# A transformer trunk on one core: the second quarter of attention goes first, filler products on both sides of the fifth block, one lasting tile of scores, adding transfers spread over stage A

## The chip, the cores and the metric

The kernel runs on one core of a Trainium2 chip. A core has four compute engines that run side by side, each with its own stream of instructions: TensorE (PE in the profile; its weight loads are PEld), VectorE (DVE), ScalarE (ACT) and GpSimd (POOL). SyncE (SP) issues most of the DMA transfers between the device's memory and the core's SBUF; GpSimd issues some. Matmul results land in PSUM. An engine takes its instructions in order, and waits on semaphores for the other engines and for transfers.

The metric is the device time of one execution in microseconds (us), as the median of several runs.

## The reference

One layer over 2048 positions of width 1024, 16 heads of 64, all float32: chunked attention with a learned position bias, then a dense SwiGLU part of width 2816, each between two RMS norms and added to the residual.

```python
def chunk_relpos_attention(h, w_qkv, w_o, rel_bias):
    """Chunked attention: chunk c attends to chunks max(0,c-8)..c."""
...
    for c in range(n_chunks):
        k0 = max(0, (c - LEFT_CHUNKS) * CHUNK)
        k1 = (c + 1) * CHUNK
...
        sc = jnp.einsum('bhqd,bhkd->bhqk', q_blk, k[:, :, k0:k1]).astype(jnp.float32) * scale
        sc = sc + bias[None, :, :, BAND - n_keys:]
        p = jax.nn.softmax(sc, axis=-1).astype(v.dtype)
        outs.append(jnp.einsum('bhqk,bhkd->bhqd', p, v[:, :, k0:k1]))
...
    return merge_heads(o) @ w_o
...
        h = rms_norm(x, g_pre_mix[i])
...
        x = x + rms_norm(m, g_post_mix[i])
        h = rms_norm(x, g_pre_ffn[i])
        x = x + rms_norm(swiglu(h, w_gate[i], w_up[i], w_down[i]), g_post_ffn[i])
```

A chunk is 64 positions (`CHUNK`) and `LEFT_CHUNKS` is 8, so 128 queries see at most 640 keys: their own 128 and the 512 before. The first 512 positions of the sequence see fewer, since nothing stands before them.

## The kernel before

Every product that needs float32 is made of three matmuls on parts of the operands (`products`, L197 to L199): one product unit is three matmuls of 128x512.

**Stage A** (`project()`, TensorE from 0 to 492 us of the profiled execution) makes v, q and k for all positions in blocks that take fewer products than a plain matrix product, at the price of sums of weights and of activations. It is a generator of 672 product units, and the main program counts them in `done`. Results q, k, v go to device memory and are fetched again by attention. Beside it the main program advances `weight_sums()`, a generator that prepares sums of the feed-forward part's down weights in device memory with 44 copies and 44 adding transfers of 256 KB: the copies (`copy`) are issued by SP, the adding ones (`add`) by GpSimd, in 60 steps. GpSimd also stores sums of weights for stage A itself (tiles `s_q_S`) and computes the norms' small powers (tiles `hr`).

**Stage B**, attention, runs from 492 to 1139.5 us. A job, `Attend(n, p)`, is a quarter n of the positions (512 queries) and a pair of heads p: 4 x 8 = 32 jobs, in the order of the list `jobs`. A job has four turns of 128 queries. Quarter n=0 sees 128, 256, 384 and 512 keys in its four turns, and the other quarters 640 in each (`self.prev`). A turn's work, by the functions that the main loop calls:
- `scores`: eight matmuls (four where there are few keys) into `st`, one tile over three PSUM banks of which there is one buffer; VectorE adds the bias and finds the row's extreme (head one, then head two), ScalarE takes the exponential of each (tiles `sc`). The loop is three turns ahead with the scores (`AHEAD`).
- `scaled`: VectorE's reciprocal of the row sums, GpSimd's scaling of `sc`.
- `transposed`: TensorE turns four 128x128 blocks of each head into a PSUM tile `tt` (two buffers); VectorE copies head one's into `pT`, ScalarE head two's.
- `fifth`: the fifth block of both heads, which only the quarters with 640 keys have, goes into a third such `tt`, copied by ScalarE.
- `output`, once per job, at the beginning of the next job's first turn: the product with v into `po`.

`load` fetches a job's q, keys, bias, and for every second pair the values v; a job with previous keys fetches those of quarter n-1 as well. It is issued behind the second block of scores of the job before it.

**Filler.** While a quarter's attention runs, `o_quarter` of the quarter before it, the product with w_o, supplies product units (64 in a quarter) that `fill(t)` takes from a generator, so much TensorE time at a time; `left` is what remains. The first quarter of attention has no filler, and the last quarter's `o_quarter` runs after attention. The main loop sets the order of all this on TensorE by hand (`manual_schedule`): the program's order is TensorE's order. On the other engines a planner orders the instructions when the kernel is built, by its own costs.

The lines that set how much filler goes where, before:

```python
        share = (0.4 if t % 4 == 0 else 1.2) * left[0] / max(per - t % per - 1, 1)
        if t > 0 and t % 4 == 0:
            fill(0.45 * share)
...
        fill((0.55 if t % 4 == 0 else 1.0) * share)
        job.fifth()
```

So a job's first turn, which also has the output product, gets a third of what the other turns get, and all filler of a turn stands ahead of its fifth block.

Of the kernel before, what the change touches and what calls it, by code (L numbers as in the profile page):

```python
# [49 lines left out]
def trunk(  # L50
# [344 lines left out]
            return [one(dt) for dt in range(KT)]  # L395

    heads = (slice(0, 64), slice(64, 128))
    phase = {}
    ats, values, osums = {}, {}, {}
    bias = {}  # L400
# [43 lines left out]
    class Attend:  # L444
# [8 lines left out]
        def load(self, begin=False):  # L453
            n, p, ap = self.n, self.p, phase.get("ap")
            if begin:
                both, rest = hb_tile(2), hb_tile(3, F32)
                self.q = both[:, 0]
                self.kk = both[:, 1].rearrange("d a c -> d (a c)").rearrange("d (h c) -> d h c", h=2)
            else:
                self.q = ap.tile([P, 4, HALF], F32R, tag="q", name=f"q_{n}_{p}", bufs=2)  # L460
                self.kk = ap.tile([P, 2, 2 * HALF], F32R, tag="k", name=f"k_{n}_{p}", bufs=2)
            src = q_d[n][p].rearrange("(h d) a c -> d h (a c)", h=2)
            for half in heads:
                sp.dma_start(self.q[half].rearrange("d (h a) c -> d h (a c)", h=2).bitcast(F32), src)
            if self.prev:
                sp.dma_start(self.kk[:, :, 0:HALF].bitcast(F32), k_d[n - 1][p])
            sp.dma_start(self.kk[:, :, HALF:].bitcast(F32), k_d[n][p])
            if begin:
                flat = rest[:, 1].rearrange("d a c -> d (a c)")
                self.bias = [bias_tile(h, h, flat[:, 640 * h : 640 * h + 640]) for h in range(2)]  # L470
            else:
                self.bias = [bias_tile(NH * n + 2 * p + h, 2 * p + h) for h in range(2)]
            if p % 2 == 0:
                here = slice(p * P, p * P + 256)
                if begin:
                    v = rest[:, 0].rearrange("d a c -> d (a c)").rearrange("d (b c) -> d b c", b=8)
                else:
                    v = ap.tile([P, 8, 256], F32, tag="v", name=f"v_{n}_{p}", bufs=2)
                if self.prev:
                    sp.dma_start(v[:, 0:4, :], v_d[n - 1][:, :, here])  # L480
                sp.dma_start(v[:, 4:8, :], v_d[n][:, :, here])
                values[n, p // 2] = v
# [7 lines left out]
        def scores(self, ib):  # L490
# [6 lines left out]
            else:  # L497
                n, k0 = (ib + 1) * P, HALF
                cuts = [(0, n), (512, 512 + n)]
            st = phase["psa"].tile([P, 3 * HALF], F32, tag="S", name="st", bufs=1)  # L500
            for h in range(2):
                c0 = cuts[h][0]
                for a, b in zip(cuts[h][:-1], cuts[h][1:]):
# [58 lines left out]
        def output(self):  # L562
            n, p = self.n, self.p
            v = values[n, p // 2]
            terms = [(0, 4, 0, HALF)]
            for r in range(1, 5 if self.prev else 4):
                if self.prev:
                    terms.append((r, r - 1, 0, r * P))
                if r < 4:
                    terms.append((r, 4 + r, r * P, HALF))  # L570
            po = phase["psa"].tile([P, HALF], F32, tag="po", name="po", bufs=1)
            for m, (r, kb, c0, c1) in enumerate(terms):
                for h in range(2):
                    c = (p % 2) * P + h * 64
                    pe.matmul(  # L575
                        po[heads[h], c0:c1], v[:, kb, c : c + 64], self.pT[:, h, r, c0:c1],
                        start=m == 0, stop=m == len(terms) - 1,
                    )
            if p == 0:
                ats[n] = Cols(((0, 1), (2, 3))[n % 2])  # L580
            act.activation(ats[n].hi(p), po, AF.Copy)
            return lambda: dve.tensor_tensor(ats[n].lo(p), po, ats[n].hi(p).bitcast(F32), op=ALU.subtract)

    def o_quarter(n):

        src = ats[n]
        last = n == NQ - 1
        osums[n] = row_tile("osum", f"osum_{n}") if n % 2 else const.tile([P, HALF], F32, name=f"osum_{n}", tag="osum", bufs=1)
        for d2 in range(KT // 2):
            w = take()  # L590
            if last and d2 == KT // 2 - 1:
# [913 lines left out]
    stack_a, stack_f = ExitStack(), [ExitStack(), ExitStack()]  # L1505
    ctx.enter_context(tc.manual_schedule(engines={mybir.EngineType.PE}))

    jobs = [Attend(n, p) for n in range(NQ) for p in range(NPAIR)]
    open_ffn(0)
    sums_, done = weight_sums(), 0.0  # L1510
    for c in project():
        tick(c / (3 * C512))
        done += c / (3 * C512)
        if done > 400.0 and done % 4.0 < 1.0:
            next(sums_, None)
    drain()
    stack_f[0].close()
# [31 lines left out]
        if t < AHEAD - 1:  # L1549
            jobs[0].scaled()  # L1550
    for t in range(slots):
        share = (0.4 if t % 4 == 0 else 1.2) * left[0] / max(per - t % per - 1, 1)
        if t > 0 and t % 4 == 0:
            fill(0.45 * share)
            low = jobs[t // 4 - 1].output()
            if t % per == 0:
                n = t // per - 1
                fill(1e9)
                drain()
                work, left[0] = o_quarter(n), KT * KT * 3 * C512  # L1560
                if n > 0:
                    later.extend(lates[n - 1].rows(1.5) + lates[n - 1].write(3.0, pool))
                if n == 2:
                    later.extend(blocks[0].sums(2.0))
        if t == 16:
# [7 lines left out]
        ahead(t + AHEAD)  # L1573
        if t > 0 and t % 4 == 0:
            low()
        fill((0.55 if t % 4 == 0 else 1.0) * share)
        job.fifth()
    jobs[-1].output()()
    fill(1e9)
    drain()  # L1580
# [90 lines left out]
```

## Time and profile before

| what | value |
|---|---|
| median of three runs | 2477.16 us (2471.22 to 2478.87) |
| the profiled execution | 2479.19 us, span of its records 2477.4 us |
| mean granted clock of TensorE | 0.986 |
| busy share of the span | TensorE 95%, VectorE 67%, ScalarE 47%, GpSimd 13% |
| memory read and written | 380.14 and 170.44 MB, 222 GB/s over the span |
| matmuls | 11480, 2356.4 us busy |

In the rows of the profile a group is named by its line, engine, operation, and by the tiles it writes and reads (`st<-k,q`); then stand its count, its busy time and mean length, and the idle time of that engine just ahead of it with what ended it. In a timeline a row is the start, the length and the instruction, with the wait ahead of it in brackets. Between one block of scores and the next on TensorE lies one turn, so the distance of two such starts is the length of a turn. The time between two starts of `po`, the output product, is a job.

### The profile page before, as it was taken

What the parts mean: (1) busy time and instruction counts of PE and PEld (TensorE: products, weight loads), DVE (VectorE), ACT (ScalarE), POOL (GpSimd) and SP (SyncE); (2) the same over time, 40 slices, a digit from 0 to 9 for tenths busy, and PEclk for the clock granted to TensorE, in tenths of its full rate; (3) what the DMA queues carried; (4) which work ended last, traced back from release to release, by engine and by line L of the source; (5) the groups of instructions that cost most, each with busy time, mean ns of one, the idle gap of its engine ahead of it and who ended that gap; (6) DMA issues with size and microseconds to landing.
All of it is one profiled execution on the core that took longest, in us unless ns stands there. A gap on an engine that the chain in (4) does not pass through costs nothing.

```text
span 2477.4 us, 33015 instructions
## 1 busy us (share of the span) xinstructions
PE 2356.4 (95%) x11480; PEld 1916.3 (77%) x11480; DVE 1651.3 (67%) x2625; ACT 1163.5 (47%) x2039; POOL 313.6 (13%) x422
## 2 busy tenths in 40 slices
PE   8999999978899899888999999999999999999998
PEld 6888788756667667666887888888888888888887
DVE  7787856656555555566877688577657657555567
ACT  7445633356555555565533343356433333334454
POOL 1000022133223323330000000000000000000002
PEclk9999999988999999999999999999999999999999
DMA  7677599999767877865567554377666757457654
GB/s 281 200 255 258 179 296 322 273 251 241 206 179 203 249 189 196 236 182 197 185 241 248 187 192 157 127 236 236 229 220 195 231 171 226 142 162 241 193 185 155
DMA packets 229782, 529.72 MB, mean 214 GB/s; under 512 B 26320, under 2 KB 42720, under 8 KB 225136
## 3 DMA queue, kind: packets, MB, share of 16 engines
q1 hardware_dynamic: 217712, 480.42, 62.3%
q0 software_dynamic: 11904, 47.19, 6.1%
q8 instruction: 91, 1.49, 0.3%
q14 instruction: 75, 0.61, 0.1%
HBM read 380.14 MB, written 170.44 MB: 222 GB/s over the span
## 4 chain that ended last, share of the span: by engine, by line
PE 54%; DVE 2%; issue 1%; ACT 1%; DMA 1%; POOL 0%; DVEq 0%; SPq 0%; POOLq 0%; ACTq 0%
PE pd L199 6%; PE pd L197 6%; PE pd L198 6%; PE pb L197 5%; PE pb L199 5%; PE pb L198 5%; PE pa L199 3%; PE pa L198 3%; PE pa L197 3%; PE pc L199 3%; PE pc L198 3%; PE pc L197 3%; PE po L575 1%; PE mm L199 1%; PE mm L197 1%
## 5 line engine op out<-in xcount | busy, mean ns | idle before, releaser
L518 ACT ACTIVATE sc<-sc,rows 128x640 f32<-128x640 f32 (+4 forms) x256 | 193.0, 755 | 126.2 <-DVE rows L514 125.9
L530 POOL TENSOR_SCALAR sc<-sc,rows 128x640 f32<-128x640 f32 (+4 forms) x256 | 192.9, 766 | 411.7 <-DVE rows L527 212.4
L514 DVE CUSTOM_DVE_ANT_0 sc<-st,bias 128x640 f32<-128x640 f32 (+2 forms) x248 | 176.1, 745 | 95.8 <-PE st L506 66.1
L197 PE MATMUL pb<-hb,w_wg_T 128*128 128x512 f32 x528 | 206.0, 390 | 2.6 <-DVE terms L963 2.6
L199 PE MATMUL pb<-hb,w_wg_T 128*128 128x512 f32 x528 | 205.7, 390 | 0.0
L198 PE MATMUL pb<-hb,w_wg_T 128*128 128x512 f32 x528 | 205.6, 389 | 0.0
L545 PE MATMUL tt<-ident,sc 128*128 128x128 f32 x928 | 144.1, 286 | 46.1 <-DVE pT L548 25.2
L545 PEld LDWEIGHTS tt<-ident,sc 128*128 128x128 f32 x928 | 107.6, 146 | 82.7 <-issue 68.8
L505 PE MATMUL st<-k,q 128*128 128x384 f32 (+3 forms) x440 | 142.8, 344 | 29.7 <-DVE rows L514 20.0
L199 PE MATMUL pd<-a,w_d_T 128*128 128x512 f32 (+1 forms) x368 | 140.0, 380 | 0.1
L197 PE MATMUL pd<-a,w_d_T 128*128 128x512 f32 (+1 forms) x368 | 140.0, 380 | 0.0
L198 PE MATMUL pd<-a,w_d_T 128*128 128x512 f32 (+1 forms) x368 | 139.9, 380 | 0.0
L197 PE MATMUL pa<-hb,w_wg_B 128*128 128x512 f32 x352 | 137.1, 389 | 0.0
L199 PE MATMUL pa<-hb,w_wg_B 128*128 128x512 f32 x352 | 137.0, 389 | 0.0
L198 PE MATMUL pa<-hb,w_wg_B 128*128 128x512 f32 x352 | 137.0, 389 | 0.0
L506 PE MATMUL st<-k,q 128*128 128x384 f32 (+3 forms) x440 | 131.7, 319 | 0.0
L965 ACT ACTIVATE terms<-terms 128x512 f32<-128x512 f32 x65 | 41.1, 632 | 181.9 <-DVE terms L963 181.9
L548 DVE COPY pT<-tt 128x512 f32<-128x512 f32 (+3 forms) x128 | 81.5, 637 | 66.6 <-PE tt L545 34.5
L131 ACT ACTIVATE w_wg_T<-raw 128x1024 fp32r<-128x1024 f32 x88 | 92.9, 1057 | 70.1 <-PE pa L199 30.8
L354 DVE TENSOR_TENSOR a<-raw_a,a 128x512 fp32r<-128x512 f32 x154 | 105.7, 694 | 28.8 <-ACT a L353 28.3
L575 PE MATMUL po<-pT,v 128*64 128x256 f32 (+3 forms) x864 | 124.6, 436 | 0.0
L289 POOL TENSOR_TENSOR rs<-ms,neg_half 128x4 f32<-128x4 f32 (+1 forms) x7 | 8.4, 1201 | 865.2 <-DVE ms L287 865.2
(265 smaller groups left out, 6226.5 us busy)
## 6 DMA issues: line engine op xcount, KB each, us to landing
raw<-in_w_gu SPq DMA_DIRECT2D x77, 512.0 KB, 4.2
q<-q SPq DMA_DIRECT2D x62, 512.0 KB, 7.5
k<-k SPq DMA_DIRECT2D x55, 512.0 KB, 9.8
s_g_S<-raw POOLq DMA_DIRECT2D x44, 512.0 KB, 3.0
raw_d<-d_S SPq DMA_DIRECT2D x88, 256.0 KB, 3.7
raw_a<-aT SPq DMA_DIRECT2D x88, 256.0 KB, 3.6
raw<-s_g_S SPq DMA_DIRECT2D x44, 512.0 KB, 4.3
bias<-ext_d SPq DMA_DIRECT2D x124, 144.0 KB, 9.9
```

The source lines that it names most:

```text
L131: act.activation(hi, raw, AF.Copy)
L197: pe.matmul(pt, a_hi, b_hi, start=first, stop=False, skip_group_check=go_on)
L198: pe.matmul(pt, a_hi, b_lo, start=False, stop=False, skip_group_check=go_on)
L199: pe.matmul(pt, a_lo, b_hi, start=False, stop=last, skip_group_check=go_on)
L354: eng.tensor_tensor(lo, src, hi.bitcast(F32), op=ALU.subtract)
L505: pe.matmul(st[:, a:b], q[:, 2 * h, cols], kk[:, h, key], start=True, stop=False)
L506: pe.matmul(st[:, a:b], q[:, 2 * h + 1, cols], kk[:, h, key], start=False, stop=True)
L514: dve.tensor_tensor_reduce(out=sc[:, :n], in0=st[:, c0 : c0 + n], in1=rev, scale=-1.0, scalar=3.0e38, op0=ALU.add, op1=ALU.min, accum_out= ...
L518: act.activation(sc[:, :n], sc[:, :n], AF.Exp, bias=nmax, scale=-1.0, accum_out=rows[:, h : h + 1])
L530: last_pool[0] = pool.tensor_scalar(sc[:, :n], sc[:, :n], rows[:, 2 + h : 3 + h], 1.0, op0=ALU.mult, op1=ALU.mult)
L545: pe.transpose(tt[:, u, :], sc[h][:, b * P : b * P + P], ident)
L575: pe.matmul(po[heads[h], c0:c1], v[:, kb, c : c + 64], self.pT[:, h, r, c0:c1], start=m == 0, stop=m == len(terms) - 1,)
```

## The change

Four things. Line numbers of the changed kernel are higher by one to eight.

1. `SEQ_OF = (1, 0, 2, 3)`: attention takes quarter n=1 first and n=0 second. Quarter n=1 now has no filler, and n=0 has n=1's `o_quarter` as filler. n=2 has n=0's, n=3 has n=2's, and n=3's runs after attention, as before. The buffers that alternated by n alternate by the place in the sequence.
2. A turn's filler: the extra factors 0.4 and 1.2 are gone, so each turn has an equal share; half of it stands ahead of the fifth block, and the other half after it, or, in a job's first turn, half ahead of the output product and half ahead of the fifth block.
3. The score tile `st` is allocated once and kept, instead of being taken anew from a pool with one buffer in each turn.
4. `weight_sums()` advances from unit 110 of stage A in every ninth unit, instead of from unit 400 in every fourth.

```diff
--- before.py
+++ after.py
@@ -395,6 +395,7 @@
             return [one(dt) for dt in range(KT)]
 
     heads = (slice(0, 64), slice(64, 128))
+    SEQ_OF = (1, 0, 2, 3)
     phase = {}
     ats, values, osums = {}, {}, {}
     bias = {}
@@ -469,7 +470,7 @@
                 flat = rest[:, 1].rearrange("d a c -> d (a c)")
                 self.bias = [bias_tile(h, h, flat[:, 640 * h : 640 * h + 640]) for h in range(2)]
             else:
-                self.bias = [bias_tile(NH * n + 2 * p + h, 2 * p + h) for h in range(2)]
+                self.bias = [bias_tile(2 * jobs.index(self) + h, 2 * p + h) for h in range(2)]
             if p % 2 == 0:
                 here = slice(p * P, p * P + 256)
                 if begin:
@@ -497,7 +498,9 @@
             else:
                 n, k0 = (ib + 1) * P, HALF
                 cuts = [(0, n), (512, 512 + n)]
-            st = phase["psa"].tile([P, 3 * HALF], F32, tag="S", name="st", bufs=1)
+            if "S" not in phase:
+                phase["S"] = phase["psa"].tile([P, 3 * HALF], F32, name="st", bufs=1)
+            st = phase["S"]
             for h in range(2):
                 c0 = cuts[h][0]
                 for a, b in zip(cuts[h][:-1], cuts[h][1:]):
@@ -577,15 +580,15 @@
                         start=m == 0, stop=m == len(terms) - 1,
                     )
             if p == 0:
-                ats[n] = Cols(((0, 1), (2, 3))[n % 2])
+                ats[n] = Cols(((0, 1), (2, 3))[SEQ_OF.index(n) % 2])
             act.activation(ats[n].hi(p), po, AF.Copy)
             return lambda: dve.tensor_tensor(ats[n].lo(p), po, ats[n].hi(p).bitcast(F32), op=ALU.subtract)
 
     def o_quarter(n):
 
         src = ats[n]
-        last = n == NQ - 1
-        osums[n] = row_tile("osum", f"osum_{n}") if n % 2 else const.tile([P, HALF], F32, name=f"osum_{n}", tag="osum", bufs=1)
+        last = n == SEQ_OF[-1]
+        osums[n] = row_tile("osum", f"osum_{n}") if SEQ_OF.index(n) % 2 else const.tile([P, HALF], F32, name=f"osum_{n}", tag="osum", bufs=1)
         for d2 in range(KT // 2):
             w = take()
             if last and d2 == KT // 2 - 1:
@@ -1505,13 +1508,13 @@
     stack_a, stack_f = ExitStack(), [ExitStack(), ExitStack()]
     ctx.enter_context(tc.manual_schedule(engines={mybir.EngineType.PE}))
 
-    jobs = [Attend(n, p) for n in range(NQ) for p in range(NPAIR)]
+    jobs = [Attend(n, p) for n in SEQ_OF for p in range(NPAIR)]
     open_ffn(0)
     sums_, done = weight_sums(), 0.0
     for c in project():
         tick(c / (3 * C512))
         done += c / (3 * C512)
-        if done > 400.0 and done % 4.0 < 1.0:
+        if done > 110.0 and done % 9.0 < 1.0:
             next(sums_, None)
     drain()
     stack_f[0].close()
@@ -1549,17 +1552,18 @@
         if t < AHEAD - 1:
             jobs[0].scaled()
     for t in range(slots):
-        share = (0.4 if t % 4 == 0 else 1.2) * left[0] / max(per - t % per - 1, 1)
+        share = left[0] / max(per - t % per - 1, 1)
         if t > 0 and t % 4 == 0:
-            fill(0.45 * share)
+            fill(0.5 * share)
             low = jobs[t // 4 - 1].output()
             if t % per == 0:
                 n = t // per - 1
                 fill(1e9)
                 drain()
-                work, left[0] = o_quarter(n), KT * KT * 3 * C512
+                work, left[0] = o_quarter(SEQ_OF[n]), KT * KT * 3 * C512
                 if n > 0:
-                    later.extend(lates[n - 1].rows(1.5) + lates[n - 1].write(3.0, pool))
+                    late = lates[SEQ_OF[n - 1]]
+                    later.extend(late.rows(1.5) + late.write(3.0, pool))
                 if n == 2:
                     later.extend(blocks[0].sums(2.0))
         if t == 16:
@@ -1573,8 +1577,10 @@
         ahead(t + AHEAD)
         if t > 0 and t % 4 == 0:
             low()
-        fill((0.55 if t % 4 == 0 else 1.0) * share)
+        fill(0.5 * share)
         job.fifth()
+        if t % 4 < 3:
+            fill(0.5 * share)
     jobs[-1].output()()
     fill(1e9)
     drain()
```

**TensorE at the beginning of attention.** Here `pb` is the last product of stage A, and `hb_19` is the tile that holds the first job's q and keys. Before:

```order
L199 MATMUL pb<-hb_17_2473,w_wq_T_3928 128x512
L505 MATMUL st<-hb_19_3912 128x128
L506 MATMUL st<-hb_19_3912 128x128
L505 MATMUL st<-hb_19_3912 128x128
L506 MATMUL st<-hb_19_3912 128x128
L505 MATMUL st<-hb_19_3912 128x256
L506 MATMUL st<-hb_19_3912 128x256
L505 MATMUL st<-hb_19_3912 128x256
L506 MATMUL st<-hb_19_3912 128x256
```

After:

```order
L199 MATMUL pb<-hb_17_2525,w_wq_T_3930 128x512
L508 MATMUL st<-hb_19_3912 128x384
L509 MATMUL st<-hb_19_3912 128x384
L508 MATMUL st<-hb_19_3912 128x256
L509 MATMUL st<-hb_19_3912 128x256
L508 MATMUL st<-hb_19_3912 128x256
L509 MATMUL st<-hb_19_3912 128x256
L508 MATMUL st<-hb_19_3912 128x384
L509 MATMUL st<-hb_19_3912 128x384
```

The first two blocks of scores, of 128 and 256 keys, have become one of 640 keys; the second such one follows it.

**TensorE around a fifth block in quarter n=2.** `mm` is the filler's PSUM tile, `L559` (`L562` after) the fifth block, `L545` (`L548`) the other eight transposes, which belong to the next turn. Before:

```order
L506 MATMUL st<-k_3_7140,q_3_7139 128x384
L197 MATMUL mm<-hb_23_5328,w_0_7152 128x512
L198 MATMUL mm<-hb_23_5328,w_0_7152 128x512
L199 MATMUL mm<-hb_23_5328,w_0_7152 128x512
L197 MATMUL mm<-hb_23_5328,w_0_7152 128x512
L198 MATMUL mm<-hb_23_5328,w_0_7152 128x512
L199 MATMUL mm<-hb_23_5328,w_0_7152 128x512
L197 MATMUL mm<-hb_23_5328,w_0_7152 128x512
L198 MATMUL mm<-hb_23_5328,w_0_7152 128x512
L199 MATMUL mm<-hb_23_5328,w_0_7152 128x512
L559 MATMUL tt<-ident,sc 128x128 x2
L545 MATMUL tt<-ident,sc 128x128 x8
L505 MATMUL st<-k_3_7140,q_3_7139 128x384
```

After:

```order
L509 MATMUL st<-k_3_7067,q_3_7066 128x384
L197 MATMUL mm<-hb_23_5646,w_0_7083 128x512
L198 MATMUL mm<-hb_23_5646,w_0_7083 128x512
L199 MATMUL mm<-hb_23_5646,w_0_7083 128x512
L562 MATMUL tt<-ident,sc 128x128 x2
L197 MATMUL mm<-hb_23_5646,w_0_7083 128x512
L198 MATMUL mm<-hb_23_5646,w_0_7083 128x512
L199 MATMUL mm<-hb_23_5646,w_0_7083 128x512
L548 MATMUL tt<-ident,sc 128x128 x8
L508 MATMUL st<-k_3_7067,q_3_7066 128x384
```

Three products ahead of the fifth block have become one ahead of it and one behind it, in front of the next turn's transposes.

**GpSimd in stage A.** `s_q_S` are stores of weight sums that stage A fetches again, `hr` is a power that a norm waits for, and `d_S` are the adding transfers of `weight_sums()`. Before:

```order
L857 DMA s_q_S_200<-raw_1396 128x1024
L857 DMA s_q_S_199<-raw_1049 128x1024
L857 DMA s_q_S_198<-raw_1096 128x1024
L1324 TENSOR_TENSOR hr<-ms,neg_half 128x4
L857 DMA s_q_S_201<-raw_1344 128x1024
L857 DMA s_q_S_203<-raw_1346 128x1024
L857 DMA s_q_S_204<-raw_1710 128x1024
L857 DMA s_q_S_202<-raw_1396 128x1024
L1324 TENSOR_TENSOR hr<-ms,neg_half 128x4
```

After:

```order
L860 DMA s_q_S_199<-raw_1050 128x1024
L798 DMA d_S_175<-in_w_d 32x2048 x2
L860 DMA s_q_S_200<-raw_1406 128x1024
L860 DMA s_q_S_198<-raw_1098 128x1024
L798 DMA d_S_176<-d_S_175 32x2048 x2
L1327 TENSOR_TENSOR hr<-ms,neg_half 128x4
L860 DMA s_q_S_201<-raw_1353 128x1024
L798 DMA d_S_177<-in_w_d 32x2048
L860 DMA s_q_S_203<-raw_1355 128x1024
L798 DMA d_S_177<-in_w_d 32x2048
L860 DMA s_q_S_202<-raw_1406 128x1024
L798 DMA d_S_175<-in_w_d 32x2048 x2
```

The adding transfers, which stood in one piece behind the last of these rows, now stand among the stores of weight sums and ahead of the powers.

## The prediction

> **What bounds the kernel now.** I read the granted clock first (one core, 0.986, so nothing is disturbed), then the busy time of each engine by stage. Columns: stretch, its length, then busy time (count) of matmuls, weight loads, VectorE, ScalarE, GpSimd, the granted TensorE clock, the share of the DMA engines in use, GB/s. The rows are stage A's second half, the start of attention up to the first output product, the rest of quarter n=0, then n=1, n=2, n=3, and the feed-forward part.
>
> ```profile
> 300.00:400.00 100.00, 100.00 (x443) 82.85 (x442) 58.01 (x75) 37.68 (x48) 21.04 (x28) 1.00 0.96 291
> 492.40:516.90 24.50, 13.10 (x49) 10.68 (x47) 11.16 (x39) 9.56 (x30) 5.54 (x12) 0.65 1.01 284
> 516.90:599.90 83.00, 65.30 (x379) 48.86 (x378) 51.02 (x177) 52.10 (x149) 29.48 (x56) 0.90 0.98 236
> 599.90:774.50 174.60, 157.40 (x1009) 122.10 (x1008) 100.40 (x216) 103.42 (x225) 55.11 (x66) 1.00 0.74 197
> 774.50:956.10 181.60, 162.40 (x1038) 125.74 (x1036) 106.99 (x224) 103.85 (x226) 64.15 (x74) 0.99 0.77 212
> 956.10:1139.50 183.40, 164.99 (x1054) 125.96 (x1054) 110.07 (x228) 108.18 (x234) 62.84 (x71) 0.99 0.72 200
> 1139.50:2477.40 1337.90, 1316.52 (x5864) 1090.38 (x5864) 920.49 (x1271) 541.50 (x819) 42.45 (x57) 0.99 0.60 200
> ```
>
> TensorE is the bound nearly everywhere: no gap at all in 300 to 400 us, 21 us of gaps in the whole feed-forward part. Only attention leaves room: 84 us of gaps in 647 us, 29 of them in the first 107 us. So attention alone is costed below. Next I listed TensorE's groups inside n=2, to see which wait ends last there (last part: idle time before the group, and what ended it):
>
> ```profile
> L545 PE MATMUL tt<-ident,sc 128*128 128x128 f32 x256 | 38.2, 277 | 15.5 <-DVE pT L548 7.8 <-ACT pT L560 3.8 <-DVE rows L527 3.0
> L505 PE MATMUL st<-k,q 128*128 128x384 f32 (+1 forms) x128 | 40.4, 337 | 3.7 <-DVE rows L514 3.7
> ```
>
> The transposes of head two hold 15.5 of that quarter's 19.2 us: with two buffers `tt` they wait until the fifth block has been copied out.
>
> **1. A full quarter without filler (n=1 now goes first).** The timeline of TensorE has turns of a full quarter into which no filler fell, so their length can be read off:
>
> ```profile
> 692.69 0.42 PE L505 MATMUL st<-k,q 128*128 128x384 f32 x1
> ...
> 695.90 0.44 PE L505 MATMUL st<-k,q 128*128 128x384 f32 x1 [0.37 <-DVE rows L514]
> ...
> 772.98 0.42 PE L505 MATMUL st<-k,q 128*128 128x384 f32 x1
> ...
> 774.55 4.53 PE L575 MATMUL po<-pT,v 128*64 128x512 f32 x32
> ...
> 779.86 0.42 PE L505 MATMUL st<-k,q 128*128 128x384 f32 x1
> ```
>
> From one block of scores to the next it is 3.21 us where TensorE waits for VectorE to read the single score tile, and 6.88 us where the output product stands between. A job (four turns) is then 3 x 3.21 + 6.88 = 16.5 us. Seven jobs after the first output product: 115.5 us. Ends: 113 (a wait less in each job) to 121 (three late loads of some 2 us, the size seen in n=0).
>
> The start gets longer, because more is fetched. Before:
>
> ```profile
> 498.19 0.58 PE L505 MATMUL st<-hb 128*128 128x256 f32 x1 [5.24 <-DVE rows L514]
> 510.12 0.45 PE L505 MATMUL st<-k,q 128*128 128x128 f32 x1 [4.12 <-DMA k<-k]
> ```
>
> The fifth block of scores (job two) waited for its keys to 510.1, with the DMA engines full. These are the DMA issues by kind: count, size of each, us to landing:
>
> ```profile
> q<-q SPq DMA_DIRECT2D x62, 512.0 KB, 7.5
> k<-k SPq DMA_DIRECT2D x55, 512.0 KB, 9.8
> bias<-ext_d SPq DMA_DIRECT2D x124, 144.0 KB, 9.9
> raw<-in_w_o SPq DMA_DIRECT2D x32, 512.0 KB, 5.3
> v<-v SPq DMA_DIRECT2D x27, 512.0 KB, 7.3
> o<-y SPq DMA_DIRECT2D x32, 256.0 KB, 2.4
> ```
>
> A job of n=1 also needs keys and, every second job, values of quarter n=0. Up to the fifth block that is three transfers of 512 KB more, 1.57 MB, at the 250 GB/s between the rows of this stretch 6.3 us: 516.4. Two cycles of 3.2 and 1.57 us from scores to output product (772.98 to 774.55) give 524.4, 32 us after the start instead of 24.5. Ends: 28 (the loads were waiting anyway) to 36 (stores of q and k, which share the queue, land as late again).
>
> **2. Quarter n=0 with filler.** A job of it without filler:
>
> ```profile
> 529.66 0.48 PE L505 MATMUL st<-k,q 128*128 128x512 f32 x1
> ...
> 532.35 0.33 PE L505 MATMUL st<-k,q 128*128 128x128 f32 x1 [1.08 <-DVE rows L514]
> ...
> 534.43 0.39 PE L505 MATMUL st<-k,q 128*128 128x256 f32 x1 [0.74 <-DVE rows L514]
> ...
> 536.13 0.45 PE L505 MATMUL st<-k,q 128*128 128x384 f32 x1
> ...
> 539.89 0.48 PE L505 MATMUL st<-k,q 128*128 128x512 f32 x1
> ```
>
> 10.23 us, 1.82 of them waits, so 8.4 us of TensorE's work. A quarter has 64 filler products, 8 a job, of 0.68 us each (three matmuls; 856.21 to 856.89 below): 5.5 us. They cover the waits for the score tile, and the job becomes TensorE's own 13.9 us, eight of them 111 us. The other limit is data. A job fetches 2 x 512 (q) + 512 (k) + 4 x 144 (bias) + 256 (v) KB, and with filler 512 (weights) and stores 256: 3136 KB, or 3.21 MB, in 13.9 us, 231 GB/s. What full DMA engines moved here:
>
> ```profile
> 500.00:510.00 10.00, 5.01 (x14) 3.64 (x14) 3.62 (x15) 4.26 (x14) 3.44 (x6) 0.67 0.98 241
> 540.00:550.00 10.00, 8.09 (x53) 5.87 (x52) 6.66 (x25) 6.71 (x21) 3.93 (x9) 1.00 1.06 245
> 560.00:570.00 10.00, 7.06 (x40) 4.93 (x38) 6.55 (x18) 6.32 (x15) 3.44 (x6) 0.84 1.06 223
> ```
>
> At 245 the data take 13.1 us a job, at 223 14.4 us. So 111 to 122 us (the latter with 1.5 MB more for the next quarter's first jobs); I take 115, nearer the lower end, since two of the three rows are above 231.
>
> **3. Filler on both sides of the fifth block.** One turn of n=2, TensorE, then ScalarE:
>
> ```profile
> 854.96 0.42 PE L505 MATMUL st<-k,q 128*128 128x384 f32 x1
> ...
> 856.21 0.39 PE L197 MATMUL mm<-hb,w 128*128 128x512 f32 x1
> ...
> 856.89 0.39 PE L197 MATMUL mm<-hb,w 128*128 128x512 f32 x1
> ...
> 857.58 0.38 PE L559 MATMUL tt<-ident,sc 128*128 128x128 f32 x2
> ...
> 859.27 0.63 PE L545 MATMUL tt<-ident,sc 128*128 128x128 f32 x4 [0.88 <-DVE pT L548]
> 859.65 0.42 PE L505 MATMUL st<-k,q 128*128 128x384 f32 x1
> ...
> 858.20 0.81 ACT L518 ACTIVATE sc<-sc,rows 128x640 f32<-128x640 f32 x1
> ...
> 859.01 0.36 ACT L560 ACTIVATE pT<-tt 128x256 f32<-128x256 f32 x1
> ```
>
> The fifth block leaves TensorE at 857.6 and is copied only at 859.0, because ScalarE has both exponentials ahead of it. The chain is scores, VectorE's reduction, two exponentials, the copy, head two's transposes: 4.7 us, whatever filler stands inside it. Moving a product behind the fifth block helps only where ScalarE's order puts the copy first. In the order of the changed kernel that is so in all turns of n=1 (which has no filler), and in 16 of the 48 turns of n=2 and n=3 that count (the three of each job not followed by the output product); before it is 10. A turn with the copy first is worth TensorE's own work, 3.8 us (4.69 less the 0.88 waited), and saves 0.9 us: 6 x 0.9 = 5.4 us. Against it, the first turn of a job now always carries two products where before it often had none and took 3.2 us; I take 1.4 us off for that. Gain 4 us of the two quarters; ends: 12 (the copy slips in between the exponentials in half of the rest) and a loss of 8 (a longer first turn in each of 16 jobs at 0.5 us).
>
> **4. The lasting score tile.** In the order each block of scores still waits once, for VectorE's second reduction, as with rotating tiles: nothing. Bounds: the whole 3.7 us of waits at L505 in a quarter (second row of the groups above) saved, or as much again lost; I take 0, which these straddle.
>
> **5. Adding transfers over stage A.** The 44 copies and 44 additions of 256 KB are the same. They move from the last 36% of the stage (units 400 to 640 of 672) to four fifths of it (110 to 650), on SP's queue (copies) and GpSimd's (additions), where the stores of weight sums and two small powers now stand behind additions. While they were dense the DMA engines were 96% in use and TensorE had no gap (first row above), so spreading them thinner gains nothing there; cover in the first half is the six tiles of weights fetched ahead. Bounds: a gain of the 4 us key wait at 510, if less were left over, against one stall per power, two of at most 6 us; I take 0: the key wait comes from attention's own loads.
>
> **The sum.** Start 32, n=1 115.5, n=0 115: 262.5 us against 24.5 + 83.0 + 174.6 = 282.1, that is 19.6 less, and 4 less in n=2 and n=3: 23.6 us. The profiled execution took 2479.2 us (span 2477.4), 2.0 above the median of the three runs: 2455.6 for a like execution, 2453.6 for the median.
>
> **Rivals.** *More gain:* filler after the fifth block hides the transposes' wait wholly in n=2 and n=3. For it: filler in the right place. Against: ScalarE's order. Some 15.5 us in each quarter go instead of 4 in both: 27 us more, 2427. *Data hold n=0:* loads of weights coincide with the keys of the next job, four jobs in eight wait 4 us (the 4.12 us above): 130 us, 2468. For it: 231 GB/s wanted of 223 to 245. Against: TensorE's slower pace leaves each load 3 us longer. *Slower, by one mechanism:* the clock falls in n=1 without filler. In 492.4 to 516.9 it was 0.65. At 0.67 throughout n=1 the work on the path (1.26 us of scores in three cycles, and the 6.88) grows by half, 5.25 us a job, 42 in all: 2495. It eats the gain from 0.78 down. Against it: 540 to 550, with transposes, waits of a microsecond and no filler, has 1.00; gaps in n=1 should be 0.4 us. *The adding transfers cost:* powers held up and weights late in the first half, 25 us of stalls wanted for no gain; against it the row at 96%.
>
> The Trainium skill, "TensorE: Matmul & The Clock Gate", section "Part 4: PE-mode transpose", says that transposes do not count as TensorE activity in the way matmuls do, so that the clock stays low. By that rule n=1 without filler, a third of it transposes, would run at half clock and cost 10.7 us more a job, about 2540. The row 540 to 550 speaks against it, and it is counted in the slower rival.
>
> **How the numbers follow.** Forecast 0.70, more gain 0.11, data hold n=0 0.09, clock 0.06, adding transfers 0.04. The ends of parts 1 to 3 reach from 42 us less to 5 more; taken together eight times in ten they give 38 to 8 less, and with the rivals 2437 to 2470. A change of 0.3% (7.4 us) is about what can be told from none: faster is the forecast, more gain and most of the data case, 0.87; within 0.3% 0.07; slower 0.06.
>
> **What would show it.** Right: score blocks 3.2 us apart in n=1 with the clock at 1.0, first output product near 524, the eighth near 640, the sixteenth near 755 (before 774.5), jobs of n=0 about 14 us, waits at the transposes still 10 us or more in n=2 and n=3, no new gaps before 492. Wrong: a clock under 0.8 in n=1, waits for k or bias at the scores of n=0 over 10 us in sum, gaps of TensorE between 100 and 490, or transposes that wait no more.

## The result, and the profile after

The changed kernel took 2446.7 us (median of 4 runs, 2438.93 to 2449.68) where the kernel before took 2478.0 (4 runs): ratio 0.9871, 95% interval 0.9839 to 0.9903. Timed again beside other kernels it had 2443.2 us (2443.05 to 2449.51) and 0.9874 (0.9854 to 0.9894). Its profiled execution took 2446.4 us, span 2444.6, 32.8 below that of before.

The table by stage of the changed kernel, columns as in the prediction: stage A's second half, the time up to the first output product, then seven jobs of n=1, eight of n=0, n=2, n=3, and the feed-forward part.

```profile
300.00:400.00 100.00, 100.00 (x443) 82.81 (x442) 59.63 (x77) 39.63 (x51) 12.38 (x16) 1.00 0.89 267
492.40:524.70 32.30, 23.72 (x125) 19.59 (x123) 19.42 (x44) 16.04 (x35) 8.10 (x11) 0.89 0.89 235
524.70:638.50 113.80, 104.29 (x717) 75.20 (x716) 72.48 (x179) 79.05 (x179) 43.19 (x57) 1.00 0.78 207
638.50:747.60 109.10, 106.86 (x637) 82.00 (x636) 69.06 (x212) 68.90 (x190) 35.83 (x65) 1.00 0.90 229
747.60:925.00 177.40, 159.64 (x1021) 123.35 (x1020) 106.55 (x226) 104.98 (x228) 67.31 (x75) 0.99 0.83 232
925.00:1104.50 179.50, 163.52 (x1058) 125.52 (x1057) 108.07 (x229) 107.86 (x234) 64.73 (x70) 0.99 0.73 204
1104.50:2444.60 1340.10, 1317.62 (x5861) 1090.41 (x5860) 920.44 (x1271) 541.72 (x819) 42.46 (x57) 0.99 0.60 199
```

Quarter n=0 is now nearly full (106.86 of 109.10 us). The turns of n=1, from TensorE's timeline:

```profile
549.77 0.45 PE L508 MATMUL st<-k,q 128*128 128x384 f32 x1 [0.37 <-DVE rows L517]
552.98 0.44 PE L508 MATMUL st<-k,q 128*128 128x384 f32 x1 [0.35 <-DVE rows L517]
556.19 0.45 PE L508 MATMUL st<-k,q 128*128 128x384 f32 x1 [0.35 <-DVE rows L517]
557.78 4.53 PE L578 MATMUL po<-pT,v 128*64 128x512 f32 x32
563.09 0.42 PE L508 MATMUL st<-k,q 128*128 128x384 f32 x1
```

They are 3.21 us apart, 6.90 with the output product. The groups of TensorE in n=2 that answer to the two shown of before:

```profile
L508 PE MATMUL st<-k,q 128*128 128x384 f32 (+1 forms) x128 | 40.2, 335 | 0.5 <-DVE rows L517 0.4
L548 PE MATMUL tt<-ident,sc 128*128 128x128 f32 x256 | 37.2, 276 | 17.3 <-DVE pT L551 6.7 <-DVE rows L530 6.0 <-ACT pT L563 4.5
```

The waits at the transposes are all still there (17.3 us, 15.5 before); those at the scores fell from 3.7 to 0.5.

Read from the first block of scores and the output products in each trace, the stages are (us; "start" is from the first scores to the first output product, "first" the seven jobs behind it, "second" the next eight; "A ends" is the start of the first scores). Single profiles scatter: with the same stage A it ended at 488.1 to 492.4 us where the adding transfers came late (before, e2, e3, e4), and at 495.2 to 502.2 in the seven profiles with the change's own spread; n=2 and n=3 together took 349.8 to 354.5 us in the six profiles with the changed kernel's order and filler. The ratio is to the kernel before timed beside each, whose median was 2475.1 to 2478.5:

| kernel | A ends | start | first | second | n=2 | n=3 | median | ratio, interval |
|---|---|---|---|---|---|---|---|---|
| before | 492.4 | 24.5 | 82.9 | 174.7 | 181.6 | 178.3 | 2475.1 to 2478.5 | 1 |
| changed | 498.7 | 26.0 | 113.8 | 109.1 | 177.4 | 174.3 | 2446.7 | 0.9871 (0.9839 to 0.9903) |
| changed, again | 495.2 | 27.0 | 113.8 | 109.9 | 176.1 | 174.8 | 2443.2 | 0.9874 (0.9854 to 0.9894) |
| e1 spread alone | 498.8 | 21.2 | 82.7 | 174.8 | 181.3 | 177.2 | 2484.2 | 1.0024 (1.0014 to 1.0035) |
| e2 no spread | 490.0 | 32.7 | 113.8 | 109.8 | 175.5 | 174.9 | 2442.8 | 0.9863 (0.9846 to 0.9880) |
| e3 order alone | 488.7 | 30.8 | 113.8 | 114.7 | 176.8 | 179.7 | 2454.4 | 0.9918 (0.9902 to 0.9935) |
| e4 filler alone | 488.1 | 23.4 | 79.0 | 175.3 | 187.3 | 173.9 | 2477.6 | 1.0004 (0.9991 to 1.0017) |
| e6 tile from the pool | 498.9 | 25.9 | 113.8 | 109.8 | 175.1 | 174.7 | 2444.8 | 0.9866 (0.9848 to 0.9885) |
| e12 even, all ahead | 499.2 | 26.1 | 113.8 | 109.1 | 179.6 | 180.0 | 2453.0 | 0.9896 (0.9881 to 0.9911) |
| e5 VectorE copies | 502.2 | 27.1 | 130.8 | 109.1 | 171.4 | 167.7 | 2450.1 | 0.9895 (0.9875 to 0.9916) |
| e9 the same, n=2, n=3 | 498.9 | 26.0 | 113.8 | 109.9 | 168.9 | 169.0 | 2435.7 | 0.9838 (0.9814 to 0.9862) |
| e7 a pause in the spread | 500.4 | 26.8 | 113.8 | 109.4 | 176.2 | 178.3 | 2445.0 | 0.9873 (0.9851 to 0.9894) |
| e10 small transfers | 488.4 | 26.5 | 113.8 | 109.1 | 175.4 | 174.7 | 2438.4 | 0.9845 (0.9829 to 0.9860) |
| e11 e9, adds from 365 | 492.4 | 29.1 | 113.8 | 109.3 | 169.5 | 167.7 | 2426.8 | 0.9791 (0.9769 to 0.9814) |

In each profile some 1338 to 1341 us of feed-forward follow behind the last output product. That of before, 1337.9, is the lowest; the 2.2 us to the changed kernel's 1340.1 are no more than this scatter.

### The profile page after: what moved, and what is told of

Same layout as the page of the kernel before. It is cut to its first block, busy times and chain, and to the rows that moved or that the text cites. A ratio compares the mean times of both kernels' runs of the same rounds, so it can differ in the third digit from the quotient of the medians.

```text
span 2444.6 us, 33016 instructions
## 1 busy us (share of the span) xinstructions
PE 2347.2 (96%) x11480; PEld 1903.1 (78%) x11480; DVE 1644.1 (67%) x2625; ACT 1163.2 (48%) x2039; POOL 316.7 (13%) x422
## 4 chain that ended last, share of the span: by engine, by line
PE 54%; DVE 2%; issue 2%; DMA 1%; ACT 1%; POOL 0%; SPq 0%; DVEq 0%; ACTq 0%; POOLq 0%
PE pd L199 6%; PE pd L198 6%; PE pd L197 6%; PE pb L197 4%; PE pb L199 4%; PE pb L198 4%; PE pc L199 3%; PE pc L198 3%; PE pc L197 3%; PE pa L198 3%; PE pa L199 3%; PE pa L197 3%; PE po L578 1%; PE mm L199 1%; PE mm L197 1%
## 5 line engine op out<-in xcount | busy, mean ns | idle before, releaser
L548 PE MATMUL tt<-ident,sc 128*128 128x128 f32 x928 | 135.0, 278 | 34.3 <-DVE pT L551 10.2
L548 PEld LDWEIGHTS tt<-ident,sc 128*128 128x128 f32 x928 | 105.1, 141 | 76.9 <-issue 45.0
L508 PE MATMUL st<-k,q 128*128 128x384 f32 (+3 forms) x432 | 137.4, 338 | 14.4 <-DVE rows L517 13.1
L509 PE MATMUL st<-k,q 128*128 128x384 f32 (+3 forms) x432 | 126.9, 314 | 0.0
L197 PEld LDWEIGHTS pb<-hb,w_wg_T 128*128 128x128 f32 x528 | 99.5, 188 | 25.8 <-issue 4.6
```

The source lines that it names most:

```text
L197: pe.matmul(pt, a_hi, b_hi, start=first, stop=False, skip_group_check=go_on)
L508: pe.matmul(st[:, a:b], q[:, 2 * h, cols], kk[:, h, key], start=True, stop=False)
L509: pe.matmul(st[:, a:b], q[:, 2 * h + 1, cols], kk[:, h, key], start=False, stop=True)
L548: pe.transpose(tt[:, u, :], sc[h][:, b * P : b * P + P], ident)
```

## The experiments

### One part at a time

**e1, the adding transfers spread, alone** (on the kernel before):

```diff
-        if done > 400.0 and done % 4.0 < 1.0:
+        if done > 110.0 and done % 9.0 < 1.0:
```

> Edit: the kernel before, with only the adding transfers spread (from unit 110, each ninth). The prediction costed this part at nothing. Theory A (the loss in stage A is the adding transfers' and nothing pays it back): the first block of scores starts at 498.5 instead of 492.4, since the loads of the second half's x come late when the DMA engines are full between 160 and 280 us; the way from there to the first output product stays 24.5 us; the time is 6 us above before, 2484. Theory B (the spread empties the queues before attention, and the start gains what stage A loses): stage A ends at 498.5 too, but the wait for keys of 4.1 us near 510 goes and the start takes 20 us; 2478 to 2480. Prediction as it stood: 2478, no gap in stage A.

Measured: 0.24% slower (0.14 to 0.35), 6 us. Stage A ends later and the start is 3.3 us shorter: something of both theories, with A's sum.

**e2, the changed kernel without the spread** (the same lines, the other way).

> Edit: the changed kernel, with the adding transfers as before (from unit 400, each fourth). Theory A: stage A ends at 492.5, the start still takes 26 us, so all after it comes 6 us sooner: 2441, a version better than both. Theory B: stage A ends at 492.5, but the start takes 32 us as the prediction had it, since the loads of the first two jobs meet the tail of the adding transfers; the first output product is at 524 as in the changed kernel, and the time is 2447.

Measured: stage A ends at 490.0, and the start takes 32.7. So it is theory B: with n=1 first, stage A's loss and the start's gain nearly cancel. By the medians the spread costs 0.4 to 4 us, and the two intervals of the ratio overlap: not told from nothing.

**e3, the order alone** (`SEQ_OF` and what follows from it; the other three parts as before).

> Edit: the kernel before, with only the order of the quarters changed (n=1 first). By the changed kernel's marks the order is worth: n=1 without filler 113.8 us from the first to the eighth output product, n=0 with filler 109 to 113 us (its turns have uneven shares here), against 24.5 + 83.0 + 174.6 for start and both quarters before. Theory A: start 26, sum 249 to 253, so 29 to 33 us less: 2445 to 2449. Theory B: start 32, 23 to 27 less: 2451 to 2455. n=2 and n=3 stay at 181.6 and 178.3 us between their output products in both.

Measured: 2454.4, by theory B's number, with a start of 30.8. n=2 took 4.8 us less than before, which no theory had.

**e4, the filler alone** (even shares and both sides of the fifth block, in the old order).

> Edit: the kernel before, with only the filler changed (even shares, half of them behind the fifth block). n=1, n=2 and n=3 have filler here. By the changed kernel's marks each such quarter takes 4 us less between its output products (177.4 and 174.3 instead of 181.6 and 178.3): three quarters 12 less, 2466. By the prediction's term (2 us a quarter): 6 less, 2472. By its rival in which filler hides the transposes' wait wholly: 45 less, 2433. By the count of turns in which ScalarE's order has the fifth block's copy ahead of the exponentials (5, 6 and 12 turns of 24 in n=1, 2, 3, against 6, 5 and 7 before, 0.9 us each): n=1 and n=2 hardly change, n=3 takes 4 to 5 less, 2473.

Measured: no difference. n=3 gains 4.4 us, n=1 nothing, and n=2 took 187.3 us in its profile with a granted clock of 0.97 and waits of up to 3.4 us at the transposes. In the new order the same edit (with the lasting tile, which e6 shows to be nothing) is worth 11.6 us: 2454.4 in e3 to 2442.8 in e2. By the table 4.9 us of this are in n=0, which has filler only in the new order, 4.8 in n=3 and 1.3 in n=2. So what differs beside n=0 is n=2 alone. What makes it slow here was not settled: it rests on one profile, and the count of turns with the copy first was right for n=1 and n=3 and not for n=2.

**e6, the score tile taken from the pool again** (the changed kernel, with the old `st = ...` line).

> Edit: the changed kernel, with the score tile taken anew from its pool in each turn, as before. The prediction: each block of scores waits for VectorE's second reduction in both ways, nothing. So 2443 to 2447, stage by stage as the changed kernel, with 6.5 us of waits at the scores in n=1. Rival (the lasting tile lets the scores of head one start before head two's reduction is done, or costs waits of its own): 3 us or more to either side in n=1, where every turn ends on this wait.

Measured: as the changed kernel, in every stage. The lasting tile does nothing.

### What of the new filler gains

**e12, even shares, all ahead of the fifth block:**

```diff
-        fill(0.5 * share)
+        fill((1.0 if t % 4 < 3 else 0.5) * share)
         job.fifth()
-        if t % 4 < 3:
-            fill(0.5 * share)
```

> Edit: the changed kernel with the even shares kept, but a turn's whole share ahead of its fifth block. ScalarE's order then has the copy ahead of an exponential in 5 of 48 turns of n=2 and n=3 instead of 19. If that copy's place is what filler behind the fifth block gains: 14 turns by 0.9 us, n=2 and n=3 together 12 us longer, 2456 to 2459. If the even shares are the gain: no difference, 2443 to 2447. n=0, which has no fifth block, stays at 109 us.

The transposes of this kernel in n=2 and in n=3, whose waits were 17.3 and 13.7 us in the changed kernel:

```profile
L548 PE MATMUL tt<-ident,sc 128*128 128x128 f32 x256 | 38.2, 277 | 21.0 <-DVE pT L551 10.8 <-ACT pT L563 7.5 <-DVE rows L530 2.6
...
L548 PE MATMUL tt<-ident,sc 128*128 128x128 f32 x256 | 38.2, 277 | 22.3 <-DVE pT L551 12.1 <-DVE rows L530 5.3 <-ACT pT L563 4.5
```

Measured: 2453.0, and n=2 and n=3 together 7.9 us longer than in the changed kernel: the place behind the fifth block gains, by 0.6 us for each of the 14 turns, not 0.9. The even shares gain in n=0 alone, which took 109.1 us here and in the changed kernel, and 114.7 with uneven shares (e3): a first turn with two products where it had fewer leaves fewer waits for the score tile (2.2 us here and in the changed kernel, the first line, against 6.8 in e3, the second). In n=2 and n=3 they do not gain: with all filler ahead these took 359.6 us with even shares and 356.5 with uneven ones (e3).

```profile
L508 PE MATMUL st<-k,q 128*128 128x256 f32 (+3 forms) x70 | 24.0, 356 | 2.2 <-DVE rows L517 2.1
```

```profile
L506 PE MATMUL st<-k,q 128*128 128x256 f32 (+3 forms) x70 | 24.1, 357 | 6.8 <-DVE rows L515 6.8
```

### Is it the copy behind two exponentials?

**e5 and e9: VectorE copies the fifth block**, in n=2 and n=3 only (e9, below), or in all quarters (e5: the last line alone, without the test):

```diff
-            act.activation(self.pT[:, :, 4, cols], tt[:, 0:2, :], AF.Copy)
+            if self.n == SEQ_OF[0]:
+                act.activation(self.pT[:, :, 4, cols], tt[:, 0:2, :], AF.Copy)
+            else:
+                dve.tensor_copy(self.pT[:, :, 4, cols], tt[:, 0:2, :])
```

> Edit: the changed kernel, with the fifth block copied by VectorE instead of ScalarE, in all quarters. Theory (what holds head two's transposes is the place of this copy behind two exponentials in ScalarE's order): in n=2 and n=3 VectorE ends its second reduction 3.1 us after the turn's first score and can copy at once, so that the copy is done at 3.45 instead of 4.4 us and a turn of 4.74 us becomes 3.9; with some 32 such turns n=2 and n=3 together take 20 to 28 us less. In n=1 ScalarE copied at 1.9 us, ahead of the exponentials, and VectorE's second reduction ends at 3.1 there too: turns of 3.2 become 3.9, 21 turns, 15 us more. Together 2435 to 2442. Rival (the waits at the transposes belong to VectorE's own chain of reduction, reciprocal and scaling): n=2 and n=3 stay as they are, VectorE has 48 us more... of which none saved: 2460 or more.

> Edit: the changed kernel, with the fifth block copied by VectorE in n=2 and n=3 only, and by ScalarE in n=1. By the same theory: n=1 stays at 113.8 us for seven jobs, n=2 and n=3 take 20 to 28 us less, so 2419 to 2427. By the rival: 2447 or more.

A turn of n=2 in the changed kernel, TensorE's transposes and ScalarE:

```profile
871.01 0.42 PE L508 MATMUL st<-k,q 128*128 128x384 f32 x1
...
872.97 0.38 PE L562 MATMUL tt<-ident,sc 128*128 128x128 f32 x2
...
875.36 0.63 PE L548 MATMUL tt<-ident,sc 128*128 128x128 f32 x4 [0.88 <-DVE rows L530]
875.75 0.42 PE L508 MATMUL st<-k,q 128*128 128x384 f32 x1
...
874.26 0.81 ACT L521 ACTIVATE sc<-sc,rows 128x640 f32<-128x640 f32 x1
...
875.07 0.36 ACT L563 ACTIVATE pT<-tt 128x256 f32<-128x256 f32 x1
```

And in e9, TensorE and VectorE:

```profile
777.52 0.42 PE L508 MATMUL st<-k,q 128*128 128x384 f32 x1
...
781.13 0.63 PE L548 MATMUL tt<-ident,sc 128*128 128x128 f32 x4 [0.16 <-DVE pT L566]
781.52 0.42 PE L508 MATMUL st<-k,q 128*128 128x384 f32 x1
...
779.82 0.82 DVE L517 CUSTOM_DVE_ANT_0 sc<-st,bias 128x640 f32<-128x640 f32 x1
...
780.57 0.42 DVE L566 COPY pT<-tt 128x256 f32<-128x256 f32 x1
```

The turn falls from 4.74 to 4.00 us (3.9 expected) and the wait from 0.88 to 0.16. (The row at 875.36 names VectorE's reciprocal as its releaser, which it does not read; the copy that these transposes need is ScalarE's, which starts at 875.07.) Only 14 of n=2's 24 turns without an output product are that short: elsewhere VectorE has other work ahead of the copy, or waits for a load (2.13 us for a bias that came at 822.4). So n=2 and n=3 take 13.8 us less in the profiles (351.7 to 337.9), and the medians are 7 to 11 apart, not 20 to 28. In e5, n=1 takes 17 us more (15 expected): its waits, 6.5 us at the scores and 3.0 at the transposes in the changed kernel, are now all at the transposes behind VectorE's copy:

```profile
L548 PE MATMUL tt<-ident,sc 128*128 128x128 f32 x224 | 34.7, 284 | 29.7 <-DVE pT L563 29.4
```

The theory holds in both directions, though n=2 and n=3 gain half to two thirds of what was expected; the rival, by which these would have stayed as they were, does not.

### What the spread costs stage A

**e7, a pause in the spread** (units 230 to 370 left out, and each fifth unit from there).

> Edit: the changed kernel, with the adding transfers kept out of units 230 to 370 of stage A, where the second half's x is fetched (units 110 to 230 each ninth, from 370 each fifth). Theory (the spread costs stage A 9 us only because it fills the DMA engines while x is fetched; the transfers gone before attention save 6 us at its start): stage A ends at 490, start 26 to 28, so 6 to 8 us less than the changed kernel, 2439 to 2441. Rival (any adding transfer in the first half costs, or they must be done by unit 650): stage A at 495 or more, or a start of 32: 2443 to 2447.

Measured: stage A ends at 500.4; the theory as put there fell. A gap of 3.9 us came at 177 us, which the changed kernel does not have, and the one at 260 us stayed (the kernel before has one there too). Thirteen steps ahead of unit 230 cost as much as all.

**e10, the same order with a thirty-second of the bytes** (`long(to)[0:2]` and `long(a)[0:2]` in `copy` and `add`). The feed-forward part then reads plain weights where it read these sums, so this kernel leaves out part of the layer; only its times are used:

> Edit: the changed kernel, with each of the 88 copies and adding transfers cut to a thirty-second of its bytes (8 KB); the feed-forward part then reads a block of the plain weights of the same size where it read these sums, so that part of the computation is left out. The order on TensorE, VectorE and ScalarE is word for word the changed kernel's. If the loss in stage A is the bytes (full DMA engines from 160 to 280 us): the 400th product at 303 to 307 us as in the kernels without the spread (310 to 317 with it), the first block of scores at 488 to 492, start 26 us; 6 to 9 us less, 2437 to 2440. If it is the order (stores and powers behind adding transfers on GpSimd's queue, copies ahead of loads on SP's, another order of VectorE's work): the first block of scores stays at 495 to 499.

Three stretches of stage A (columns as in the prediction), of before, of the changed kernel, and of e10:

```profile
160.00:200.00 40.00, 40.00 (x180) 33.15 (x179) 31.16 (x41) 17.36 (x25) 3.23 (x5) 1.00 0.78 259
200.00:240.00 40.00, 40.00 (x179) 32.88 (x178) 27.45 (x35) 17.89 (x26) 1.67 (x3) 1.00 0.76 249
240.00:280.00 40.00, 36.28 (x147) 29.10 (x146) 37.78 (x58) 28.70 (x47) 0.00 (x0) 0.91 0.58 194
```

```profile
160.00:200.00 40.00, 40.00 (x180) 33.12 (x179) 30.48 (x40) 19.29 (x28) 7.78 (x11) 1.00 1.01 324
200.00:240.00 40.00, 37.78 (x169) 31.00 (x168) 27.49 (x36) 14.28 (x20) 11.25 (x15) 1.00 0.99 304
240.00:280.00 40.00, 32.17 (x128) 24.88 (x127) 33.72 (x53) 28.94 (x48) 3.08 (x4) 0.91 0.93 298
```

```profile
160.00:200.00 40.00, 40.00 (x180) 33.12 (x179) 29.65 (x38) 18.94 (x28) 7.68 (x11) 1.00 0.78 261
200.00:240.00 40.00, 40.00 (x179) 32.90 (x178) 31.61 (x42) 20.96 (x31) 10.41 (x14) 1.00 0.87 283
240.00:280.00 40.00, 36.93 (x156) 30.12 (x155) 38.39 (x59) 27.75 (x46) 5.35 (x7) 0.96 0.62 201
```

The DMA engines were 0.76 to 0.78 in use between 160 and 240 us before, and full with the spread; with the same order of instructions and few bytes they were at 0.78 and 0.87. Of TensorE's gaps only the one near 256 us is left, 3.07 us long, which the kernel before has too (3.45), and stage A ends at 488.4. So it is the bytes, not the order. ScalarE's longest wait for x of the second half, between 190 and 275 us, shows one way in: 3.2 us before, then 9.1 in the changed kernel. In e1 it is 8.6, and e10 shows none.

```profile
ACT hb L1291 <- DMA hb<-in_x: 3.2, 1, 3.2
```

```profile
ACT hb L1294 <- DMA hb<-in_x: 9.1, 1, 9.1
```

The start of 26.5 us in e10, where no adding bytes are left, is the changed kernel's: its spread leaves nothing behind for the start.

**e11, e9 with the adding transfers from unit 365, each fourth**:

> Edit: the kernel with VectorE's copy of the fifth block in n=2 and n=3, and the adding transfers from unit 365 of stage A in every fourth, after the second half's x has come and 35 units sooner than in the kernel before. If adding transfers in the first half are what costs stage A its 9 us, and their tail at the start of attention 6: stage A ends at 490, start 26 to 28, 2427 to 2430, 7 less than the same kernel with the spread (2435.7). If either half of that fails: 2433 to 2436.

Measured: 2426.8 us, 2.1% (1.9 to 2.3) faster than before and the fastest of all here. Stage A ends at 492.4 and the start takes 29.1, so the start's part is half had.

**e8, the changed kernel again**, for the comparison with e2:

> The changed kernel as it is, timed beside the others: 2447. With the adding transfers as before it had 2442.8 by another call's runs; here it should stand 3 to 5 us above that.

It had 2443.2, so the difference that this expected did not show.

## Why the prediction was right, point by point

The time, 2446.7 against 2453.6, came out right; of its six terms two were right (n=1, the lasting tile), one nearly (the filler), one gained 6 us more than forecast (n=0), and two missed by some 6 us in opposite directions (the start, the adding transfers), which cancelled by luck. A gain of 3.4 us in n=2 and n=3 from the order alone had no term.

**n=1 without filler: right.** 16.53 us a job (16.5 predicted), 113.8 us for seven (115.5). The last is 14.0, since it already makes the light first scores of n=0.

**The clock in n=1: the rival fell.** The granted clock is 1.00 from 524.7 to 638.5 us, although the transposes of the two heads alone, without the fifth block's, are 32.9 of 104.3 us of TensorE's work there. That the gate holds the clock low for transposes, as the Trainium skill's "TensorE: Matmul & The Clock Gate", section "Part 4: PE-mode transpose", would have it, is not seen where matmuls stand between them; by that rule it would have been some 2540, by the prediction's estimate.

**n=0 with filler: 109.1 instead of 115.** Data did not hold it: 229 GB/s at a share of 0.90, and no wait for keys or bias. TensorE's own 13.9 us a job were the limit (13.6 measured), and the step from 111 to 115 for data was the error. The kernel before had 11.8 us a job in n=0 without filler and 21.8 in n=1 with it, so the same eight products cost 1.8 us a job in n=0 and 5.3 in n=1 (21.8 less 16.5): this is what the order gains, some 28 us in eight jobs. The 115 stands in e3, but for another reason, the uneven shares, which the prediction left out of this part.

**The start: 26.0 instead of 32, by a cause the prediction had in another part.** With the adding transfers as before it is 30.8 (e3) and 32.7 (e2), so the size was right for that. Its place was not: the fifth block waits 1.2 us for keys, not the 10 that 516.4 implied; what grew is the wait of the second block for VectorE's first reduction, shown here for the changed kernel and for e2 (before: 5.24), each with a row of VectorE:

```profile
503.36 0.44 PE L508 MATMUL st<-hb 128*128 128x384 f32 x1 [3.29 <-DVE rows L517]
...
501.13 0.69 DVE L436 SCALAR_TENSOR_TENSOR lo<-terms,hi 128x512 fp32r<-128x512 f32 x1 [0.70 <-ACT hi L435]
```

```profile
499.74 0.69 PE L508 MATMUL st<-hb 128*128 128x384 f32 x1 [8.38 <-DVE rows L517]
...
513.58 0.39 PE L508 MATMUL st<-k,q 128*128 128x256 f32 x1 [1.22 <-DMA k<-k]
...
494.87 0.69 DVE L436 SCALAR_TENSOR_TENSOR lo<-terms,hi 128x512 fp32r<-128x512 f32 x1 [3.24 <-DMA q<-hi]
```

VectorE has last splits of stage A's results (`lo`) ahead of that reduction. When the first scores begin, three are left in e2, the first of which waits 3.24 us for a store of q, with the DMA engines at 1.06 from 490 to 500 us; in the changed kernel one has just begun and one more is left, with a share of 0.66 there.

**The adding transfers: nothing predicted, and two things of 6 us that cancel.** The step that failed is "While they were dense the DMA engines were 96% in use and TensorE had no gap (first row above), so spreading them thinner gains nothing there; cover in the first half is the six tiles of weights fetched ahead." The row, of 300 to 400 us, was read where the transfers had been, not where they went: there the engines had 0.22 to 0.24 left, no more, and the cover did not hold. TensorE waits 10.2 us between 100 and 492 us where it waited 4.5 before (gaps of 0.82 at 136 and 3.45 at 258), a sign that the prediction had named for being wrong, and stage A ends 6.3 us later. That the tail of these transfers reached into attention's start stood as a bound (4 us); it was 4 to 7 (30.8 and 32.7 against 26.0 and 27.0). The first output product at 524.7, predicted "near 524", was right by these two errors, that is by luck.

**Filler on both sides: 8.2 us less in n=2 and n=3, 4 predicted; the order has a part in it.** The mechanism was right (e12, e5, e9), with the waits at the transposes still 17.3 and 13.7 us, so the rival in which they go wholly fell. Of the 8.2 us, 3.4 come with the order alone (n=2 and n=3 together 359.9 us before, 356.5 in e3), which was not explained. The filler itself then gains 4.8 us (351.7 in the changed kernel) to 6.1 (350.4 in e2). Both parts of the term were too small: the place behind the fifth block gains 7.9 us (e12) where 5.4 were put, and the even shares lose 3.1 (e12 against e3) where 1.4 were taken off; the eight first turns of n=2 grew from 30.7 to 35.9 us in sum. Differences of 3 us are within the scatter of such profiles.

**The lasting tile: nothing, right** (e6).

## What to carry to other kernels

Give the filler to the stage that leaves TensorE the most idle time. Here that is n=0, idle in 17.7 of 83.0 us without filler, and not n=1, idle in 9.5 of 113.8: 282 us of two quarters and their start became 249 although no work was removed. Before spreading transfers, look at the DMA share of the stretch that they move to, not of the one that they leave; a cut to a thirty-second of their bytes, in the same order, tells bandwidth from order in one run. And two terms that cancel make a right total: check a forecast by its marks, and by what each of them consists of.

## What the hardware showed that was not expected

A gap of TensorE costs more than its length where the clock falls behind it, and whether it falls is not a matter of the gap's length alone. These are two gaps of about the same length, in the changed kernel (with the clock of a slice of 4 us behind it) and in e11 (the slice begins with the last 1.1 us of the gap):

```profile
215.10 0.47 PE L197 MATMUL pb<-hb,w_wq_T 128*128 128x512 f32 x1 [2.21 <-DVE terms L1249]
...
216.00:220.00 4.00, 4.00 (x20) 3.29 (x19) 4.00 (x6) 0.97 (x2) 1.01 (x2) 1.00 1.12 301
...
262.00:266.00 4.00, 3.75 (x9) 2.35 (x8) 4.00 (x6) 3.54 (x7) 0.39 (x1) 0.52 0.97 218
```

```profile
409.09 0.47 PE L197 MATMUL pb<-hb,w_wq_T 128*128 128x512 f32 x1 [2.08 <-DVE terms L1252]
...
408.00:412.00 4.00, 2.91 (x8) 2.32 (x9) 3.27 (x6) 1.58 (x2) 1.49 (x2) 0.69 1.02 352
```

Behind 2.21 us the clock stayed at 1.00, behind 2.08 the slice has 0.69; behind the 4.47 us gap at 260 it has 0.52 (last row of the first fence). In slices of half a microsecond the clock is 1.00 or 0.50, apart from those in which it changes, and stays at 0.50 for 3.4 us in e11 (from 409.5) and for 6.8 us around 260. In all these profiles, from 90 us to the end of stage A, the shortest gap with a fall behind it is 1.90 us (e6, at 265.9) and the longest without one 2.88 us (e1, at 214.1); every gap of 3.07 us or more had one. The Trainium skill, "TensorE: Matmul & The Clock Gate", section "HAM oscillation — how this bites in real kernels", gives the rule as no idle gaps over about 3.4 us; the 4.47 us gap agrees with it, and the 2.08 us one does not.
